# Gate and up tiles of the feed-forward block by pairs, in seven block products instead of eight

## The chip, the cores and the metric

One core of a Trainium2 chip. TensorE (PE) multiplies and writes to PSUM, VectorE (DVE) and ScalarE (ACT) read PSUM and SBUF, GpSimd (POOL) works from SBUF to SBUF, SyncE (SP) issues most of the DMAs. Each engine runs its own list of instructions in order and waits at semaphores. The metric is the device time of one execution in microseconds (us), as the median of several runs.

## The reference

Two layers of a diffusion backbone over 640 tokens (128 context, 512 latent) with 1024 channels and 2816 hidden channels. What the change touches is the second half of a layer; everything is float32.

```python
def trunk_layer(x, cond, layer_idx, p, rope, ctx):
    mod = jnp.einsum('bd,de->be', jax.nn.silu(cond), p['w_mod']) + p['b_mod']
    sh1, sc1, g1, sh2, sc2, g2 = jnp.split(mod[:, None, :], 6, axis=-1)
    h = rms_norm(x, p['norm1']) * (1 + sc1) + sh1
    ...
    x = x + g1 * (merged @ p['w_out'])
    h2 = rms_norm(x, p['norm2']) * (1 + sc2) + sh2
    ff = (jax.nn.silu(h2 @ p['w_ff_gate']) * (h2 @ p['w_ff_up'])) @ p['w_ff_down']
    x = x + g2 * ff
```

## The kernel before, in words

Activations lie channels by tokens: a tile is 128 channels by 640 tokens. A float32 product is made of three products in the type fp32r: a high part (a rounding cast) and a low part (the rest) of weight and activation, as wh·xh + wh·xl + wl·xh (`acc3`, L391 to L393). The tokens go in two parts, `SPLIT`: columns 0 to 383 and 384 to 639.

Weights come as units of 128x1024 (eight blocks of 128x128 along the 1024 inputs of one output tile). SP loads a unit into `raw`; `split_weight` has ACT cast it to `wh` (L362) and POOL subtract to `wl` (L366), in halves of 512 columns. There are four `wh` and four `wl` tiles of 1024. A unit's tiles come free when PE has made its last product (`used`), and only then is the next unit split.

A layer is the mixer (three branches), the product with `w_out` and the norm of its result, and the FFN (`ffn`). The FFN runs in three parts of 8, 7 and 7 hidden tiles (`FF_PARTS`). In a part each hidden tile takes a gate unit and an up unit, each 2 token parts by 8 blocks by 3 matmuls; ACT takes tanh (L1312), DVE multiplies (L1313, L1315, which read PSUM) and splits the result into `ah` and `al` (L383 on ACT, L384 on DVE). Then the part's product with `w_ff_down` is added to `x2` in SBUF by DVE (L1181). The first four units of a stage are made for the first token part by blocks, in four PSUM banks (`units` with `ahead`, L412), while the second token part is being normalized.

PE's list is in program order. Those of DVE, ACT and POOL are ordered by a scheduler when the program is built. Side work is fed in by `slot`, which counts the columns that PE has done. Such work is `mod_next`: it computes the modulation vector on DVE, two passes (L577) over each 128x512 tile of `w_mod`. Layer 0's runs in layer 0's mixer, the whole of layer 1's in layer 0's FFN. At the start of the program a part of it is made on PE instead (`mod_first`, L533).

## Time and profile before

| | us |
|---|---|
| median of 3 runs (2382.84 to 2386.67) | 2385.02 |
| the profiled execution | 2385.45 |
| its span, first to last instruction | 2383.7 |

The page gives each engine's busy time as a share of the span: PE 95%, DVE 59%, POOL 40%, ACT 37%. PE's records overlap, as matmuls are pipelined, so the time of one is the distance from start to start. PEclk is the granted TensorE clock: 1.00 is the upper of its two levels (2.4 GHz), 0.50 the lower (1.2 GHz). A blank between two engines' work is put down to the instruction that ended it.

### The profile page before, as it was taken

To read this page: it belongs to the slowest core of one execution; us is meant where nothing else is said; L and a number is where in the kernel's file an instruction comes from. 1 tells how busy PE (TensorE), PEld (TensorE's weight loads), DVE (VectorE), ACT (ScalarE), POOL (GpSimd) and SP (SyncE) were. 2 spreads that over 40 slices of the span, in tenths; PEclk is the share of its full clock that TensorE was granted. 3 is DMA by queue.
4 is the path that set the end of the run, shared out by engine and by line. 5 is a ranking of instruction groups with operands and counts; after the bars stand their busy time and mean duration, and the time that the engine had idled before them with its cause. 6 is when DMAs were issued, how large, how long until landed. Compare 5 with 4: busy or idle time off the path is not lost.

```text
span 2383.7 us, 42638 instructions
## 1 busy us (share of the span) xinstructions
PE 2273.8 (95%) x17060; PEld 2233.6 (94%) x17060; DVE 1417.8 (59%) x3062; ACT 879.6 (37%) x2008; POOL 956.2 (40%) x795
## 2 busy tenths in 40 slices
PE   6989899999998999999989999999999999999999
PEld 4888899999897999999979999999999989999999
DVE  5897887676956695887464657857724442222222
ACT  3444446464233322212234554464634332122221
POOL 1343644443334433444333545534333343333332
PEclk9999999999998999999999999999999999999999
DMA  7443221212511353444322222212123122222222
GB/s 286 145 130 101 79 68 53 67 54 95 198 63 54 137 177 106 151 150 149 99 101 71 79 72 72 67 48 64 48 80 112 58 71 72 80 71 73 79 80 71
DMA packets 90309, 228.25 MB, mean 96 GB/s; under 512 B 12416, under 2 KB 20480, under 8 KB 90112
## 3 DMA queue, kind: packets, MB, share of 16 engines
q1 hardware_dynamic: 85504, 218.69, 27.4%
q10 hardware_dynamic: 4608, 6.85, 0.9%
q8 instruction: 134, 2.20, 0.4%
q14 instruction: 63, 0.52, 0.1%
HBM read 213.96 MB, written 6.82 MB: 93 GB/s over the span
## 4 chain that ended last, share of the span: by engine, by line
PE 48%; DVE 7%; ACT 1%; POOL 1%; issue 1%; DMA 0%; ACTq 0%; SPq 0%; DVEq 0%; POOLq 0%
PE main L391 14%; PE main L392 14%; PE main L393 14%; PE big L412 1%; PE big L1068 1%; PE misc L1119 1%; DVE junk L577 1%; PE big L776 1%; DVE w L1000 1%; DVE ht L650 1%; DVE rs_t L472 0%; PE misc L1099 0%; DVE tg L1158 0%; DVE rs_t L473 0%; POOL ek L855 0%
## 5 line engine op out<-in xcount | busy, mean ns | idle before, releaser
L366 POOL TENSOR_TENSOR wl<-raw,wh 128x512 fp32r<-128x512 f32 x552 | 763.9, 1405 | 1142.0 <-ACT wh L362 1105.1
L362 ACT CAST wh<-raw 128x512 fp32r<-128x512 f32 x556 | 329.7, 618 | 505.2 <-PE main L392 265.4
L391 PE MATMUL main<-h2h,wh 128*128 128x256 f32 (+1 forms) x1344 | 413.2, 307 | 0.3 <-DVE tt L1313 0.3
L393 PE MATMUL main<-h2h,wl 128*128 128x256 f32 (+1 forms) x1344 | 412.8, 307 | 0.0
L392 PE MATMUL main<-h2l,wh 128*128 128x256 f32 (+1 forms) x1344 | 412.8, 307 | 0.0
L577 DVE SCALAR_TENSOR_TENSOR junk<-rawm,cond 128x512 bf16<-128x512 f32 x320 | 288.5, 902 | 37.8 <-DMA rawm<-in_w_modt_dram 33.1
L391 PE MATMUL main<-hh,wh 128*128 128x384 f32 (+1 forms) x960 | 302.4, 315 | 6.2 <-DVE rx L1200 3.5
L392 PE MATMUL main<-hl,wh 128*128 128x384 f32 (+1 forms) x960 | 297.1, 309 | 0.0
L393 PE MATMUL main<-hh,wl 128*128 128x384 f32 (+1 forms) x960 | 297.0, 309 | 0.0
L391 PEld LDWEIGHTS main<-h2h,wh 128*128 128x128 f32 x1344 | 254.6, 189 | 0.9 <-DVE tt L1313 0.5
L392 PEld LDWEIGHTS main<-h2l,wh 128*128 128x128 f32 x1344 | 254.7, 190 | 0.0
L393 PEld LDWEIGHTS main<-h2h,wl 128*128 128x128 f32 x1344 | 254.6, 189 | 0.0
L391 PE MATMUL main<-wh,hh 128*128 128x256 f32 x800 | 234.3, 293 | 5.7 <-ACT tm L461 4.0
L392 PE MATMUL main<-wl,hh 128*128 128x256 f32 x800 | 228.4, 286 | 0.0
L393 PE MATMUL main<-wh,hl 128*128 128x256 f32 x800 | 228.3, 285 | 0.0
L391 PE MATMUL main<-ah,wh 128*128 128x384 f32 (+1 forms) x704 | 219.9, 312 | 8.1 <-DVE x L1181 7.5
L392 PE MATMUL main<-al,wh 128*128 128x384 f32 (+1 forms) x704 | 218.4, 310 | 0.0
L393 PE MATMUL main<-ah,wl 128*128 128x384 f32 (+1 forms) x704 | 218.3, 310 | 0.0
L1181 DVE SCALAR_TENSOR_TENSOR x<-main,g,x 128x256 f32<-128x256 f32 (+1 forms) x192 | 78.0, 435 | 208.1 <-PE main L393 208.0
L391 PEld LDWEIGHTS main<-hh,wh 128*128 128x128 f32 x960 | 184.2, 192 | 6.9 <-DVE rx L1200 3.7
L392 PEld LDWEIGHTS main<-hl,wh 128*128 128x128 f32 x960 | 184.6, 192 | 0.1
L393 PEld LDWEIGHTS main<-hh,wl 128*128 128x128 f32 x960 | 184.2, 192 | 0.0
(276 smaller groups left out, 4698.2 us busy)
## 6 DMA issues: line engine op xcount, KB each, us to landing
raw<-in_w_dram SPq DMA_DIRECT2D x276, 512.0 KB, 3.3
rawm<-in_w_modt_dram SPq DMA_DIRECT2D x160, 256.0 KB, 4.4
rawm<-in_w_mod_dram SPq DMA_DIRECT2D x32, 256.0 KB, 5.5
x<-in_x_t_dram SPq DMA_DIRECT2D x12, 320.0 KB, 6.3
cond<-in_cond_b_dram SPq DMA_DIRECT2D x12, 256.0 KB, 4.8
qds<-qd SPq DMA_DIRECT2D x16, 160.0 KB, 2.6
x<-xd SPq DMA_DIRECT2D x8, 320.0 KB, 5.0
states<-state SPq DMA_DIRECT2D x16, 128.0 KB, 3.8
```

The source lines that it names most:

```text
L362: nc.scalar.copy(h[:, c], raw)
L366: (nc.vector if late else nc.gpsimd).tensor_sub(lo[:, c], raw, h[:, c].bitcast(F32))
L391: nc.tensor.matmul(ps, wh, xh, start=(i == 0), stop=False)
L392: nc.tensor.matmul(ps, wh, xl, start=False, stop=False)
L393: nc.tensor.matmul(ps, wl, xh, start=False, stop=(i == n - 1))
L412: self.nc.tensor.matmul(self.banks[i], a, b, start=(k == 0 and n == 0), stop=(k == KT - 1 and n == 2))
L577: nc.vector.scalar_tensor_tensor(self.sm([P, 512], "junk", 1, mybir.dt.bfloat16), raw, 1.0, cond[i, k], op0=ALU.mult, op1=ALU.mult, accum_ ...
L650: nc.vector.tensor_scalar_add(t[:, c], t[:, c], shift)
L776: nc.tensor.matmul(ps[64 * x : 64 * x + 64, o : o + 64], kk[r, ks], qq[r, qs], start=True, stop=True)
L1000: nc.vector.tensor_mul(hv(wm)[:, :, a, b], hv(x[:, 1:])[:, :, a, 1 - b], hv(sn)[:, :, a, b])
L1068: nc.tensor.matmul(S[:, x], q[:, c : c + P], k, start=(y == 0), stop=(y == 1))
L1181: nc.vector.scalar_tensor_tensor(x[:, r], ps[:, r.start - s.start : r.stop - s.start], g[:, m, i : i + 1], x[:, r], op0=ALU.mult, op1=ALU.add)
```

## The change

A gate unit and its up unit are taken together as a block matrix with two rows (gate, up: blocks A11, A12 and A21, A22, each 128 outputs by 512 inputs), and the activations as one with two columns (two token halves: B11, B21 and B12, B22). The product of the two takes eight block products; the change makes seven, in the form with sums S1 = A21+A22, S2 = S1-A11, S3 = A11-A21, S4 = A12-S2 of the weights and T1 = B12-B11, T2 = B22-T1, T3 = B22-B12, T4 = B21-T2 of the activations. For that

- the tokens are cut in equal halves of 320 everywhere, and the FFN runs in four parts of 6, 6, 5 and 5 hidden tiles; the first two hidden tiles of a layer stay as before, the other 20 are pairs (`seven`);
- weights are loaded and split in halves of 512 columns, with eight `wh` and eight `wl` tiles of that size. DVE makes S1 to S4 from the raw halves (`source`, L385, L387, L391, L398), S3 in place of A21 and S4 in place of S2; each of the seven blocks is cast by ACT (L412) and subtracted by POOL (L413);
- products of a pair are added up in PSUM where they can be, and otherwise through copies by ACT (L502, L505) and sums by DVE (L508, L514, L515, L519, L523) in tiles `e`;
- the norm keeps its result in float32 in place of x (`norm_keep`), and `combine` makes T1 to T4 and their high and low parts (L762 to L767 and L437). x itself goes to DRAM (`xd`) after `w_out`, and every part of the FFN loads it, adds and stores it;
- layer 1's modulation is cut in two. Its first part runs on PE in layer 0's FFN (`mod_later`, with `mod_first`), the rest by `mod_next` in layer 1's mixer, as layer 0's does in its own.

```diff
-FF_PARTS = ((0, 8), (8, 7), (15, 7))
-SPLIT = (slice(0, 384), slice(384, T))
-STILES = ((0, 1, 2), (3, 4))
+FF_PARTS = ((0, 6), (6, 6), (12, 5), (17, 5))
+HT = T // 2
+SPLIT = (slice(0, HT), slice(HT, T))
...
+PRODUCTS = ("A11", "S1", "S2", "A12", "S3", "S4", "A22")
...
-        self.wr = pool("wr", 2)
-        self.wh = pool("wh", 4)
-        self.wl = pool("wl", 4)
+        self.wr = pool("wr", 4)
+        self.wh = pool("wh", 8)
+        self.wl = pool("wl", 8)
...
+    def source(self, g, p):
+        nc = self.nc
+        if p in (0, 1):
+            return self.raws.pop((g, p)), 1
+        r = lambda u, i: self.raws[g + u, i]
+        if p == "A11":
+            s1 = self.sums["S1"] = self.unit("s")[:, :512]
+            nc.vector.tensor_add(s1, r(1, 0), r(1, 1))
+            nc.vector.tensor_sub(r(1, 0), r(0, 0), r(1, 0))
+            return r(0, 0), 0
+        if p == "S1":
+            s2 = self.sums["S2"] = self.unit("s")[:, :512]
+            nc.vector.tensor_sub(s2, self.sums["S1"], self.raws.pop((g, 0)))
+            return self.sums.pop("S1"), 1
+        if p in ("S2", "S4"):
+            return self.sums[p] if p == "S2" else self.sums.pop(p), 0
+        if p == "A12":
+            s4 = self.sums["S4"] = self.sums.pop("S2")
+            nc.vector.tensor_sub(s4, r(0, 1), s4)
+            return self.raws.pop((g, 1)), 1
+        return self.raws.pop((g + 1, 0 if p == "S3" else 1)), 1
...
+        key = self.jobs.popleft()
+        raw, free = self.source(*key)
+        h = self.wh.tile([P, 512], F32R, tag="wh", name=self.name("wh"))
+        lo = self.wl.tile([P, 512], F32R, tag="wl", name=self.name("wl"))
+        self.ws[key] = h, lo
+        nc.scalar.copy(h, raw)
+        low = lambda: (nc.vector if late else nc.gpsimd).tensor_sub(lo, raw, h.bitcast(F32))
         if late:
             return low
         low()
-        self.load_weight()
+        self.load_weight(free)
...
+    def seven(self, l, u, act, tmp):
+        nc = self.nc
+        g = l * N_UNITS + u
+        (e1, e16), (e5, u3) = ([t[:, s] for s in SPLIT] for t in tmp)
+        def product(ps, w, x, more):
+            h, lo = self.ws[g, w]
+            c = lambda k: slice(k * P, (k + 1) * P)
+            self.acc3(ps, [(h[:, c(k)], lo[:, c(k)], *act[x][k]) for k in range(4)], more)
+            self.used(l, u, w)
+        a, b, c = self.main()[:, :HT], self.main()[:, :HT], self.big()[:, :HT]
+        product(a, "A11", "B11", False)
+        nc.scalar.copy(e1, a)
+        self.slot(HT // 2)
+        product(b, "S1", "T1", False)
+        nc.scalar.copy(e5, b)
+        self.slot(HT // 2)
+        product(c, "S2", "T2", False)
+        nc.vector.tensor_add(e16, c, e1)
+        self.slot(HT // 2)
+        product(a, "A12", "B21", True)
+        yield 0, 0, a
+        self.slot(HT // 2)
+        product(c, "S3", "T3", True)
+        nc.vector.tensor_add(u3, c, e1)
+        nc.vector.tensor_add(e5, e5, u3)
+        yield 1, 1, e5
+        self.slot(HT // 2)
+        product(b, "S4", "B22", True)
+        nc.vector.tensor_add(e16, e16, b)
+        yield 0, 1, e16
+        self.slot(HT // 2)
+        product(c, "A22", "T4", True)
+        nc.vector.tensor_add(e1, e1, c)
+        yield 1, 0, e1
...
+    def mod_later(self, l, small, mod, scale1):
+        for c in range(4):
+            raws = []
+            first = self.mod_first(raws, c, small, mod, scale1)
+            for ks in (range(4), range(4, KT)):
+                raws += self.mod_load(c, l, ks)
+                yield
+                for _ in ks:
+                    next(first, None)
+                yield
+            for _ in first:
+                pass
...
+    def norm_keep(self, xs, rb, scale, mod, shift0, p, out):
+        nc = self.nc
+        s = SPLIT[p]
+        conds = ((0, slice(0, TC)), (1, slice(TC, HT))) if p == 0 else ((1, slice(0, HT)),)
+        for x in range(KT + 1):
+            if x < KT:
+                t = xs[x][:, s]
+                for i, c in conds:
+                    nc.vector.scalar_tensor_tensor(t[:, c], t[:, c], scale[:, x, i : i + 1], rb[:, c], op0=ALU.mult, op1=ALU.mult)
+                for i, c in conds:
+                    nc.scalar.activation(t[:, c], t[:, c], AF.Identity, bias=mod[:, shift0 + x, i : i + 1])
+                nc.scalar.copy(out[x][0][:, s], t)
+            if x >= 1:
+                (nc.vector if x % 2 else nc.gpsimd).tensor_sub(out[x - 1][1][:, s], xs[x - 1][:, s], out[x - 1][0][:, s].bitcast(F32))
...
+        t12, t4 = self.pairs("t", 4), self.pairs("t", 2)
+        act = {x: [] for x in ("B11", "T1", "T2", "B21", "T3", "B22", "T4")}
+        with self.tc.manual_schedule(engines={mybir.EngineType.DVE, mybir.EngineType.Activation}):
+            for k in range(4):
+                x, y, t = xs[k], xs[k + 4], self.unit("tf")
+                nc.vector.tensor_sub(t[:, s0], x[:, s1], x[:, s0])
+                nc.vector.tensor_sub(t[:, s1], y[:, s1], t[:, s0])
+                nc.scalar.copy(t12[k][0], t)
+                nc.gpsimd.tensor_sub(t12[k][1], t, t12[k][0].bitcast(F32))
+                nc.vector.tensor_sub(x[:, s1], y[:, s1], x[:, s1])
+                nc.vector.tensor_sub(y[:, s0], y[:, s0], t[:, s1])
+            for k in range(4):
+                x, y = xs[k], xs[k + 4]
+                d = [z[:, SPLIT[k % 2]] for z in t4[k // 2]]
+                self.split(x[:, s1], h2[k][0][:, s1], h2[k][1][:, s1])
+                self.split(y[:, s0], *d)
+                act["T4"].append(d)
...
+                    self.back, self.rate = back, 1600
+            for f in range(f, n):
+                act[f], tt = self.pairs("a", 1)[0], self.unit("tt")
+                late = {}
+                for row, p, ps in self.seven(l, u + 2 * f, act2(), [self.unit("e") for _ in range(2)]):
+                    if row == 0:
+                        gated(tt, SPLIT[p], ps)
+                    else:
+                        late[p] = ps
+                    for q in [q for q in late if (row, p) in ((0, q), (1, q)) and (q == 0 or row == 0)]:
+                        times(tt, SPLIT[q], late.pop(q), f)
...
+            def load(m):
+                if m < KT:
+                    xs[m] = self.unit("x2")
+                    nc.sync.dma_start(xs[m], self.xd[m * P : (m + 1) * P])
+            for m in range(KT if last else 2):
+                load(m)
...
+                elif p:
+                    nc.scalar.dma_start(self.xd[m * P : (m + 1) * P], xs.pop(m))
+                    load(m + 2)
...
-            mg, x2 = self.mixer(l, h, small, [self.mod_next(0, a, b, small, mod) for a, b in ((16, 36), (36, 48))] if l == 0 else None)
+            if l:
+                small, mod = later[l - 1]
+            mg, x2 = self.mixer(l, h, small, [self.mod_next(l, a, b, small, mod) for a, b in ((16, 36), (36, 48))])
...
+                nc.scalar.dma_start(self.xd[m * P : (m + 1) * P, s], x2[m][:, s])
...
-            self.ffn(l, h2, x2, g2, done, self.mod_next(l + 1, 0, 48, small, mod))
-            h = keep[1]
+                    self.queue(self.modulate(x2, acc, scale1, n_mod, 0, int(s.start > 0), keep[0]))
+            self.ffn(l, h2, act2, g2, done, self.mod_later(l + 1, n_small, n_mod, scale1))```

How it moves instructions is shown at three places. The first is VectorE's list in the middle of a part of layer 1's FFN, before: two hidden tiles. `tt` is the gated tile, `main` a PSUM bank.

```order
L1313 SCALAR_TENSOR_TENSOR tt_3799_23931<-tg_3800_23932,main_3798_23906 128x384
L1313 SCALAR_TENSOR_TENSOR tt_3799_23931<-tg_3802_23960,main_3801_23935 128x256
L1315 TENSOR_TENSOR tt_3799_23931<-tt_3799_23931,main_3806_23971 128x384
L384 TENSOR_TENSOR al_3741_23385<-tt_3799_23931,ah_3740_23384 128x384
L1315 TENSOR_TENSOR tt_3799_23931<-tt_3799_23931,main_3807_23999 128x256
L384 TENSOR_TENSOR al_3741_23385<-tt_3799_23931,ah_3740_23384 128x256
```

VectorE's list at the like place now (a pair of layer 0's first part; the pairs of both layers read alike). `e_1815` belongs to the pair before, `e_1843` to this one, `s` and `raw` are weights of the next one, and `big` is the PSUM bank of the third, fifth and seventh product.

```order
L523 TENSOR_TENSOR e_1815_9505<-e_1815_9505,big_1819_9509 128x320 [waits PE_49]
L1470 TENSOR_TENSOR tt_1798_9445<-tt_1798_9445,e_1815_9505 128x320 [waits DVE_49]
L437 TENSOR_TENSOR al_1797_9444<-tt_1798_9445,ah_1796_9443 128x320 [waits Activation_49]
L385 TENSOR_TENSOR s_1837_9642<-raw_1828_9565,raw_1831_9584 128x512 [waits DMAHW1_49,DMAHW0_49]
L437 TENSOR_TENSOR al_1797_9444<-tt_1798_9445,ah_1796_9443 128x320 [waits Activation_49]
L387 TENSOR_TENSOR raw_1828_9565<-raw_1823_9528,raw_1828_9565 128x512 [waits DMAHW7_49,DVE_49,Pool_49]
L391 TENSOR_TENSOR s_1848_9673<-s_1837_9642,raw_1823_9528 128x512
L398 TENSOR_TENSOR s_1848_9673<-raw_1836_9622,s_1848_9673 128x512 [waits DMAHW2_49,Pool_49]
L508 TENSOR_TENSOR e_1843_9656<-big_1847_9660,e_1843_9656 128x320 [waits PE_49]
L1467 SCALAR_TENSOR_TENSOR tt_1842_9655<-tt_1842_9655,main_1845_9658 128x320 [waits Activation_49]
```

Four weight sums and the PSUM sums now stand between the tile's own operations. L398 waits for POOL, and L508, the first that this pair needs, stands behind it.

The second place is TensorE's list in a pair: the end of the fourth product (A12 into `main_1845`) and the start of the fifth (S3 into `big_1847`).

```order
L443 MATMUL main_1845_9658<-h2h_1667_8454,wh_1826_9561 128x320
L443 MATMUL main_1845_9658<-h2l_1668_8455,wh_1826_9561 128x320
L443 MATMUL main_1845_9658<-h2h_1667_8454,wl_1827_9562 128x320
L443 MATMUL big_1847_9660<-h2h_1653_8440,wh_1829_9580 128x320 [waits DVE_49]
L443 MATMUL big_1847_9660<-h2l_1654_8441,wh_1829_9580 128x320
```

Before, each hidden tile's matmuls followed each other into fresh banks:

```order
L393 MATMUL main_3801_23935<-h2h_3490_21153,wl_3778_23706 128x256
L391 MATMUL main_3806_23971<-h2h_3476_21139,wh_3782_23769 128x384
L392 MATMUL main_3806_23971<-h2l_3477_21140,wh_3782_23769 128x384
L393 MATMUL main_3806_23971<-h2h_3476_21139,wl_3783_23770 128x384
L391 MATMUL main_3806_23971<-h2h_3478_21141,wh_3782_23769 128x384
```

The fifth product adds to a bank that DVE must first have read (L508), and so waits for it. ScalarE's list in the same pair, where `s_1848` is S2 of the next pair:

```order
L412 CAST wh_1849_9675<-s_1837_9642 128x512 [waits DVE_49,PE_49,Pool_49]
L502 COPY e_1843_9656<-main_1845_9658 128x320 [waits PE_49]
L505 COPY e_1844_9657<-main_1846_9659 128x320 [waits PE_49]
L412 CAST wh_1852_9694<-s_1848_9673 128x512 [waits DVE_49,Pool_49]
L412 CAST wh_1854_9712<-raw_1836_9622 128x512 [waits DMAHW2_49,PE_49,Pool_49]
```

The cast of S2 waits for its sum on DVE (L391 above). The third place is VectorE's list at the first pair of a layer: L762 to L767 are `combine`, and L1470 here waits for the last product ahead of the pairs.

```order
L763 TENSOR_TENSOR tf_1811_9460<-x2_1589_8068,tf_1811_9460 128x320 [waits DVE_49]
L1470 TENSOR_TENSOR tt_1766_9276<-tt_1766_9276,main_1789_9402 128x320 [waits PE_49]
L766 TENSOR_TENSOR x2_1585_8064<-x2_1589_8068,x2_1585_8064 128x320
L767 TENSOR_TENSOR x2_1589_8068<-x2_1589_8068,tf_1811_9460 128x320 [waits DVE_49]
L437 TENSOR_TENSOR al_1768_9278<-tt_1766_9276,ah_1767_9277 128x320 [waits Activation_49]
L762 TENSOR_TENSOR tf_1812_9467<-x2_1586_8065 128x320
```

Fourteen of `combine`'s sixteen sums, eight more `al` operations, one `al` of the tile before and one weight sum stand behind that L1470 and ahead of the first pair's L508.

## Rows read from the trace of the kernel before

**Rows 1.** Page: busy time of each engine (share of the span, x instructions).

```profile
PE 2273.8 (95%) x17060; PEld 2233.6 (94%) x17060; DVE 1417.8 (59%) x3062; ACT 879.6 (37%) x2008; POOL 956.2 (40%) x795
```

**Rows 2.** Windows: FFN of layer 0, of layer 1, gate and up there.

```profile
core 0: us, PE busy (x) PEld busy (x) DVE busy (x) ACT busy (x) POOL busy (x), PEclk, DMA share, GB/s
735.66:1229.60 493.94, 476.10 (x3184) 472.39 (x3183) 335.49 (x734) 128.50 (x263) 201.91 (x150) 0.99 0.38 129
1906.05:2380.40 474.35, 468.84 (x3176) 468.12 (x3174) 120.92 (x250) 113.69 (x231) 175.22 (x143) 0.99 0.22 75
2085.00:2183.50 98.50, 98.50 (x675) 98.50 (x674) 22.34 (x41) 26.77 (x55) 36.65 (x28) 1.00 0.23 75
```

**Rows 3.** Groups of instructions: busy us, mean ns | idle before, released by.

```profile
L366 POOL TENSOR_TENSOR wl<-raw,wh 128x512 fp32r<-128x512 f32 x552 | 763.9, 1405 | 1142.0 <-ACT wh L362 1105.1 <-issue 27.5 <-PE big L1010 7.8
L362 ACT CAST wh<-raw 128x512 fp32r<-128x512 f32 x556 | 329.7, 618 | 505.2 <-PE main L392 265.4 <-issue 188.7 <-PE main L393 22.7
...
L1315 DVE TENSOR_TENSOR tt<-tt,main 128x384 f32<-128x384 f32 x40 | 22.0, 551 | 66.3 <-PE main L393 66.3
L1315 DVE TENSOR_TENSOR tt<-tt,main 128x256 f32<-128x256 f32 x44 | 18.4, 419 | 28.3 <-PE main L393 28.1
```

**Rows 4.** Single lines: duration in ns, min/median/max, and forms.

```profile
L384 DVE TENSOR_TENSOR al<-tt,ah x88: 411/786/1496, 763.9 to 2332.8; 128x384 fp32r<-128x384 f32 x44, 128x256 fp32r<-128x256 f32 x44
L384 DVE TENSOR_TENSOR fl<-f,fh x8: 822/825/826, 90.8 to 1304.3; 128x640 fp32r<-128x640 f32 x8
L366 POOL TENSOR_TENSOR wl<-raw,wh x552: 1259/1296/1992, 21.5 to 2356.4; 128x512 fp32r<-128x512 f32 x184
L1181 DVE SCALAR_TENSOR_TENSOR x<-main,g,x x192: 341/473/486, 676.8 to 2380.6; 128x256 f32<-128x256 f32 x128, 128x128 f32<-128x128 f32 x64
```

**Rows 5.** Timeline of POOL and DVE from 125 us: start, duration.

```profile
125.03 0.69 DVE L577 SCALAR_TENSOR_TENSOR junk<-rawm,cond 128x512 bf16<-128x512 f32 x1
125.16 6.89 POOL L366 TENSOR_TENSOR wl<-raw,wh 128x512 fp32r<-128x512 f32 x4 [10.00 <-ACT wh L362]
...
125.76 1.66 DVE L577 SCALAR_TENSOR_TENSOR junk<-rawm,cond 128x512 bf16<-128x512 f32 x1
...
127.46 1.66 DVE L577 SCALAR_TENSOR_TENSOR junk<-rawm,cond 128x512 bf16<-128x512 f32 x1
```

**Rows 6.** Windows around three waits of PE (columns as in rows 2).

```profile
1892.70:1897.18 4.48, 0.28 (x4) 0.08 (x2) 4.24 (x11) 1.14 (x2) 2.70 (x3) 0.82 0.38 118
1897.18:1902.43 5.25, 5.25 (x20) 4.64 (x21) 3.90 (x13) 2.31 (x6) 0.91 (x2) 0.50 0.28 99
1911.30:1916.20 4.90, 0.30 (x3) 0.04 (x1) 4.55 (x10) 0.83 (x2) 3.75 (x7) 0.99 0.32 107
1916.20:1922.90 6.70, 6.70 (x22) 6.70 (x23) 2.20 (x12) 0.00 (x0) 0.00 (x0) 0.50 0.01 4
252.70:257.21 4.51, 0.06 (x2) 0.00 (x1) 4.51 (x5) 1.06 (x3) 2.85 (x2) 0.62 0.36 87
257.21:260.62 3.41, 3.41 (x16) 3.41 (x17) 3.41 (x6) 2.98 (x6) 1.47 (x1) 0.50 0.02 5
```

**Rows 7.** Windows: both mixers from their fifth unit, then both layers' first down products.

```profile
59.40:671.50 612.10, 577.08 (x4725) 566.78 (x4725) 483.44 (x1056) 284.06 (x686) 262.04 (x217) 0.98 0.30 98
1257.65:1841.60 583.95, 570.51 (x4725) 561.08 (x4725) 355.83 (x747) 280.47 (x677) 251.06 (x218) 0.99 0.22 72
859.20:922.10 62.90, 57.85 (x387) 56.52 (x387) 43.90 (x109) 9.43 (x17) 22.87 (x16) 1.00 0.41 140
2028.70:2085.00 56.30, 56.30 (x386) 56.30 (x386) 10.52 (x25) 9.45 (x17) 20.43 (x16) 1.00 0.23 76
```

**Rows 8.** Timeline of PE at the start, where L533 runs between other products.

```profile
38.64 0.33 PE L412 MATMUL big<-hh,wl 128*128 128x384 f32 x1
38.90 0.42 PE L533 MATMUL misc<-rawm,cond 128*32 128x128 f32 x8
39.26 0.45 PE L412 MATMUL big<-hh,wh 128*128 128x384 f32 x1
```

More of the change, by code (lines that the diff above doesn't have):

```diff
@@ L361, in split_weight @@
-        for raw, c in parts:
-            nc.scalar.copy(h[:, c], raw)
-        def low():
-            for raw, c in parts:
-                (nc.vector if late else nc.gpsimd).tensor_sub(lo[:, c], raw, h[:, c].bitcast(F32))
+        key = self.jobs.popleft()
[4 more added lines that the diff above has]
+        nc.scalar.copy(h, raw)
@@ new lines, in combine @@
+    def combine(self, xs, h2):
+        nc = self.nc
+        s0, s1 = SPLIT
+        t12, t4 = self.pairs("t", 4), self.pairs("t", 2)
[15 more added lines that the diff above has]
+                act["T4"].append(d)
+        for k in range(4):
+            for name, pair, s in (
+                ("B11", h2[k], s0), ("T3", h2[k], s1), ("B21", h2[k + 4], s0), ("B22", h2[k + 4], s1), ("T1", t12[k], s0), ("T2", t12[k], s1)
+            ):
+                act[name].append([z[:, s] for z in pair])
+        return act
@@ L1296, in mixer, with ffn @@
         return mg, x2
[L1298 removed]
+    def ffn(self, l, h2, act2, g2, done, back=None):
         nc = self.nc
@@ L1302, in ffn @@
         for fp, (_, n) in enumerate(FF_PARTS):
[L1303 to L1316 removed]
+            last = fp == len(FF_PARTS) - 1
@@ new lines, in ffn, with gated, times @@
+            act = {}
+            def gated(tg, s, ps):
+                nc.scalar.activation(tg[:, s], ps, AF.Tanh, scale=0.5)
+                nc.vector.scalar_tensor_tensor(tg[:, s], tg[:, s], 1.0, ps, op0=ALU.add, op1=ALU.mult)
+            def times(tg, s, ps, f):
+                nc.vector.tensor_mul(tg[:, s], tg[:, s], ps)
+                self.split(tg[:, s], act[f][0][:, s], act[f][1][:, s])
+            f = 0
+            if fp == 0:
+                tt = {}
+                for i, ps, s in self.units(l, range(u, u + AHEAD), h2, AHEAD):
+                    f = i // 2
+                    if i % 2 == 0:
+                        if s.start == 0:
+                            tt[f], act[f] = self.unit("tt"), self.pairs("a", 1)[0]
+                        gated(tt[f], s, ps)
+                    else:
+                        times(tt[f], s, ps, f)
+                f = AHEAD // 2
+                if back is not None:
+                    self.back, self.rate = back, 1600
```

193 lines of the change are left out of this document (103 added, 90 removed).

## The prediction

> **What bounds the kernel now.** I read the page first: PE is busy for 95% of the span, every other engine for at most 59% [rows 1]. Then the windows by stage. In layer 1's gate and up products PE has no idle time at all, and POOL and DVE do 37 and 22 us of work in 98.5 us [rows 2]. The window holds seven hidden tiles, 7 x 96 = 672 matmuls of 320 columns in the mean, so one takes 0.1466 us. There, only fewer matmuls or PE kept waiting can change the time. Next I looked for what the new work will run on. The groups and single lines give the durations [rows 3, 4], and the timeline shows how DVE and POOL meet [rows 5]: a DVE operation with both inputs in SBUF takes 0.69 us alone, and 1.66 while POOL subtracts; POOL's four subtractions then take 1.72 each instead of 1.29. They take turns. An `al` operation of 256 columns runs from 411 ns to 1496, while L1181, which reads PSUM, never takes over 486 ns [rows 4]. So a DVE operation of two SBUF inputs that finds POOL at work waits about 1.0 us (1.66 - 0.69; 1.50 - 0.42), and one that reads PSUM does not wait.
>
> **The change part by part.**
>
> *Matmuls removed.* Twenty pairs a layer, each with 12 matmuls fewer (84 for 96): 480 x 0.1466 = **-70.3 us**. A pair takes 14.07 us before and 12.31 after, if PE never waits; its seven products take 1.76 each. (The Trainium skill, "TensorE: Matmul & The Clock Gate", section "Back-to-back issue gap", gives the distance as columns / 2.4 GHz + 2.5 ns. That is 135.8 ns for 320 columns, and by it the term would be -65.2 us; the row is 11 ns longer, so the row decides.)
>
> *Work added to a pair.* POOL now subtracts seven halves instead of four, 7 x 1.29 = 9.0 us [rows 4]. DVE gets four weight sums of 512 columns (0.69 each) and five sums of 320. From 0.42 for 256 and 0.55 for 384 I take 0.49 for 320, whatever is read [rows 3], if nothing is in the way. No engine's own sum exceeds 12.3 us. What matters is the order.
>
> *The chain in a pair.* PE's fifth product adds to a bank that DVE must have read (L508). On DVE, L508 stands behind all of this since the seventh product of the pair before: L523, L1470, two `al`, L385, L387, L391, L398. And L398 overwrites S2, so it waits for POOL's subtraction of S2, which waits for ACT's cast, which waits for L391. From the end of the last product: L523, L1470 and two `al` 4 x 0.49, the sums L385, L387 and L391 3 x 0.69, together 4.0; cast 0.62; POOL 1.29; L398 0.69; L508 0.49; some eight hand-overs between engines at an estimated 0.1: 7.9 us. PE has four products to do meanwhile, 7.0 us. Without any turn lost to POOL the wait is 0.9 us a pair, and that is the lower bound. With turns lost: of the seven DVE operations ahead of the cast, six have two SBUF inputs, while POOL has the next pair's A11 and S1 to subtract; two lost turns, 2.0 us. The third is at L398: when S2 is done, the cast of A12 behind it is done too, and POOL goes on with it while L398 is being released; 1.0 more. Sum 10.9 us, less 7.0: **3.8 us** that PE waits. The upper bound, with a fourth lost turn or a weight that lands late, is 5. The order of instructions has this chain 12 times a layer (2, 4, 3 and 3 in the four parts, where two more pairs follow whose weights must be made); 24 x 3.8 = **+91 us**. (The Trainium skill, "SBUF — State Buffer", section "SBUF: two separate sides", calls the shared pair of ports an exclusive lock, held for a whole instruction by whichever starts first. The trace agrees on the lock. A wait that starts anywhere in a subtraction of 1.29 us would last 0.65 in the mean, and by that 3.8 would be 2.8 and the term +67; the rows show 1.0, as POOL tends to be just starting.)
>
> *The clock after each wait.* PE waited 4.5, 4.9 and 4.5 us in three places, and the granted clock was 0.50 for 5.25, 6.7 and 3.4 us behind that [rows 6]. Half of these is lost: 1.7 to 3.3 us. A wait of 3.8 is near those, so I take 2.0 (bounds 0 and 3.3): 24 x 2.0 = **+48**.
>
> *First and last pairs of a part.* Six more pairs (the first of a part) have only the end of the chain, from the second product on: copy 0.45, cast 0.62, POOL 1.29, L398 0.69, L508 0.49 and hand-overs against PE's 3.5; 0.4 or, with a lost turn, 1.4. I take 0.9: **+5**. At a part's end, L523, L1470, cast and `al` with one lost turn and hand-overs are 3.2 us, of which the next product's earlier blocks cover 1.8 to 2.2: 1.2 x 8 = **+10** (bounds 4 and 16). Before, these products ran without idle time in layer 1 [rows 7].
>
> *The first pair of a layer.* Behind the L1470 that ends the units ahead, DVE has 23 operations of 0.49, one of 0.69, and L508: 12.9 us with L1470 itself. With seven lost turns (the weights of four units and four of `combine`'s own subtractions come due on POOL) 19.9, less 7.0: 12.9 and a clock loss of 2.0, **+30** for both layers. Bounds: 11 without lost turns, 46 if POOL's longer subtractions each cost a turn.
>
> *Modulation moved.* In layer 0's mixer, where L577 runs, the same stretch took 612.1 us; in layer 1's, without it, 584.0 [rows 7]. Now it runs in both: I take **+25** of the 28 (bounds 15 and 30). Layer 0's FFN loses it: its first down products took 62.9 us against 56.3. I count this difference for two of the three parts, **-12** (the third part's end also has the next norm). In its place 32 groups of L533 go to PE. At the start such a group lies between two matmuls that begin 0.62 us apart instead of 0.17 [rows 8], and the next is late too; 0.55 each, **+18**, less where they fall into a wait.
>
> *Norms.* Equal halves give the first half's norm more cover (96 matmuls of 320 columns, 14.1 us, for 11.5) and the second half's less (14.1 for 16.6), and `norm_keep` has fewer DVE operations. PE waits 4.5 and 4.9 us there [rows 6]: **-6** for both layers (bounds 0 and -8). x through DRAM I cost at nothing: DMA is at 0.22 of its share in layer 1's FFN [rows 2], and tiles are asked for two ahead of use; if that cover is gone, PE waits for a landing in each down part.
>
> *Sum:* -70.3 + 91 + 48 + 5 + 10 + 30 + 25 - 12 + 18 - 6 = +139. The profiled execution took 2385.45 us (span 2383.7, 1.75 outside it), 0.4 over the median: 2385.45 + 139 = **2524 us**.
>
> **The rivals.** *Turns are not lost where I put them (faster).* If DVE's chain falls between POOL's subtractions, the wait is 0.9, the clock stays up, and the ends and the first pairs cost their lower bounds: -70 + 22 + 0 + 4 + 11 + 20 - 12 + 18 - 8 = -15, 2370 us. It speaks for it that the subtraction waits for the cast in 1105 of its 1142 idle us [rows 3], so POOL is not always there; against it, that POOL must now work 9 of 12.3 us. It decides where the wait falls below about 1.5 us a pair.
> *The chain is shorter, and the clock stays up.* Two us a pair: -70 + 48 + 3 + 8 + 24 + 25 + 6 - 6 = +38, 2423 us. For it: L385 stands ahead of L523 in three pairs, and the scheduler may have left L391 early; against it, the wait at L398.
> *All bounds are high.* 5.0 and 3.3 a pair: -70 + 199 + 8 + 14 + 46 + 28 + 8 = +233, 2618 us. For it: a raw half can only be loaded when its buffer is free, and the last sums would then wait for a landing.
> *The waits come, but the clock stays up.* Shorter waits of PE in other places may leave it at 1.00; then the sum is 139 - 48 = +91, 2476 us. Against it stand all three rows [rows 6]. It lies in my own case's range.
>
> **How the numbers follow.** My forecast (waits of 3 to 4.5 us, with or without a part of the clock loss, 2460 to 2580 us) has 0.52; the shorter chain 0.2; all high 0.12; the faster case 0.12; 0.04 lies between it and the shorter chain, of which 0.03 within 0.2% of 2385, which is about what a measurement of this kernel can tell from no change. So faster 0.12, same 0.03, slower 0.85. The range goes from the shorter chain's low side, 2405, to the high case, 2615, and leaves out some 0.2.
>
> **What would show it.** In the changed profile, right: the distance of pairs in the middle of a part is 16 to 19 us, at a part's end 12.3 to 13; PE's fifth product waits for DVE L508, and L508's predecessor L398 for POOL; DVE operations of 512 columns show 0.69 and 1.7; the clock is 0.50 in slices of the FFN; layer 1's FFN takes about 530 us and its mixer 610. Wrong: pairs at 12.3 to 13.5 us throughout, L398 without a wait, a clock of 1.00 in the FFN, or layer 1's mixer at 584.

## The result and the profile after

The changed kernel takes 2534.67 us (median of 4 runs, 2533.32 to 2536.93), the kernel before, beside it, 2383.93: ratio 1.0631, 95% interval 1.0613 to 1.065. That is slower, 11 us above the forecast of 2524.

The page, busy time of each engine and the granted clock by slices (compare [rows 1]):

```profile
PE 2289.4 (90%) x16858; PEld 2225.4 (88%) x16858; DVE 1668.8 (66%) x3362; ACT 1028.6 (41%) x2272; POOL 1132.7 (45%) x903
...
PEclk9999999999998999999989999999999989899999
```

The windows of both FFNs, then of layer 1's and layer 0's mixer from the fifth unit (compare [rows 2, 7]), columns as there:

```profile
735.59:1286.60 551.01, 482.14 (x3210) 467.06 (x3209) 305.65 (x513) 194.75 (x389) 278.71 (x206) 0.93 0.36 117
1991.54:2529.90 538.36, 468.15 (x2940) 457.24 (x2938) 291.22 (x465) 180.53 (x356) 268.99 (x197) 0.93 0.30 100
1311.86:1929.40 617.54, 584.63 (x4726) 571.69 (x4725) 474.64 (x1045) 289.52 (x688) 266.70 (x225) 0.97 0.29 92
56.50:675.00 618.50, 580.99 (x4726) 569.58 (x4725) 479.76 (x1059) 289.70 (x689) 261.80 (x219) 0.98 0.31 99
```

The FFNs are longer by 57 and 64 us, layer 1's mixer by 34, layer 0's by 6. Some 12 us come back outside these windows, mostly in the two `w_out` products and at the mixers' starts. PE is idle in 70 us of each FFN, and the clock there fell from 0.99 to 0.93.

A pair in layer 1's second part: of DVE's timeline an L1470 and the stretch from L387 to L508, POOL's and ACT's beside it, then PE.

```profile
2165.15 1.07 DVE L1470 TENSOR_TENSOR tt<-tt,e 128x320 f32<-128x320 f32 x1
...
2167.55 0.68 DVE L387 TENSOR_TENSOR raw<-raw,raw 128x512 f32<-128x512 f32 x1
2168.15 1.78 DVE L391 TENSOR_TENSOR s<-s,raw 128x512 f32<-128x512 f32 x1
2172.02 1.73 DVE L398 TENSOR_TENSOR s<-raw,s 128x512 f32<-128x512 f32 x1 [2.09 <-POOL wl L413]
2173.68 0.48 DVE L508 TENSOR_TENSOR e<-big,e 128x320 f32<-128x320 f32 x1
...
2168.03 1.35 POOL L413 TENSOR_TENSOR wl<-s,wh 128x512 fp32r<-128x512 f32 x1 [2.16 <-ACT wh L412]
2170.72 1.27 POOL L413 TENSOR_TENSOR wl<-s,wh 128x512 fp32r<-128x512 f32 x1 [1.33 <-PE main L443]
2171.94 2.94 POOL L413 TENSOR_TENSOR wl<-raw,wh 128x512 fp32r<-128x512 f32 x2
...
2170.02 0.62 ACT L412 CAST wh<-s 128x512 fp32r<-128x512 f32 x1 [1.41 <-DVE s L391]
...
2174.21 0.64 PE L443 MATMUL big<-h2h,wh 128*128 128x320 f32 x1 [3.50 <-DVE e L508]
```

L391 loses a turn to POOL (1.78 for 0.68), ACT casts the sum at 2170.02, POOL subtracts S2 until 2171.99, and only then does L398 begin, which loses the next turn to POOL's A12 (1.73). L508 ends at 2174.16, and PE, idle for 3.50 us, starts its fifth product at 2174.21. (The profile puts POOL's 1.33 us ahead of S2 down to a PE product, whose modelled end falls just there; the cast ended at 2170.64, and for the same wait in an earlier pair, at 2062.96, the profile names the cast.) The waits of the whole execution (us in total, times, longest) have one such line for PE and one for L398:

```profile
PE big L443 <- DVE e L508: 82.5, 24, 3.8
...
DVE s L398 <- POOL wl L413: 90.8, 40, 6.1
...
DVE s L385 <- DMA raw<-in_w_dram: 28.8, 13, 3.1
DVE x L1337 <- DMA x<-xd: 17.9, 7, 3.0
```

Three windows: that wait, what follows it, and the rest of the pair.

```profile
2170.71:2174.21 3.50, 0.01 (x2) 0.00 (x1) 2.19 (x3) 1.30 (x3) 3.49 (x3) 0.97 0.23 75
2174.21:2177.61 3.40, 3.40 (x13) 3.40 (x14) 0.34 (x1) 0.06 (x1) 0.68 (x1) 0.53 0.48 154
2177.61:2182.80 5.19, 5.19 (x37) 5.19 (x36) 3.69 (x7) 2.74 (x5) 3.91 (x3) 1.00 0.07 21
```

In the 3.40 us at the lower clock PE starts 13 matmuls where 23 would fit, a loss of 1.5 us; in other pairs it was 6.8 us, a loss of 2.4 to 2.9. This pair has a distance of 17.53 us to the next; a pair without the wait takes 12.32.

### The profile page after: what moved, and what is told of

The parts are those of the page before. It is cut to its first block, busy times and chain, and to the rows that moved or that the text cites. A ratio compares the mean times of both kernels' runs of the same rounds, so it can differ in the third digit from the quotient of the medians.

```text
span 2533.3 us, 44691 instructions
## 1 busy us (share of the span) xinstructions
PE 2289.4 (90%) x16858; PEld 2225.4 (88%) x16858; DVE 1668.8 (66%) x3362; ACT 1028.6 (41%) x2272; POOL 1132.7 (45%) x903
## 4 chain that ended last, share of the span: by engine, by line
PE 57%; DVE 21%; issue 7%; POOL 5%; DMA 4%; ACT 3%; SPq 0%; ACTq 0%; POOLq 0%; DVEq 0%
PE main L443 40%; PE big L443 9%; DVE junk L682 6%; POOL wl L413 3%; DMA raw<-in_w_dram 2%; PE big L1224 2%; DVE s L398 2%; PE misc L1275 1%; DMA x<-xd 1%; POOL ek L1011 1%; DVE w L1156 1%; ACT wh L412 1%; PE big L932 1%; PE misc L1255 1%; DVE mod L686 1%
## 5 line engine op out<-in xcount | busy, mean ns | idle before, releaser
L413 POOL TENSOR_TENSOR wl<-raw,wh 128x512 fp32r<-128x512 f32 x552 | 770.7, 1406 | 901.3 <-ACT wh L412 783.4
L412 ACT CAST wh<-raw 128x512 fp32r<-128x512 f32 x556 | 340.0, 620 | 448.9 <-PE main L443 378.1
L443 PE MATMUL main<-hh,wh 128*128 128x320 f32 x960 | 304.0, 317 | 2.9 <-DVE aT L1394 2.9
L443 PE MATMUL main<-hl,wh 128*128 128x320 f32 x960 | 299.8, 312 | 4.5 <-POOL hl L804 4.1
L443 PE MATMUL main<-hh,wl 128*128 128x320 f32 x960 | 298.7, 311 | 0.0
L413 POOL TENSOR_TENSOR wl<-s,wh 128x512 fp32r<-128x512 f32 x120 | 163.7, 1364 | 217.3 <-ACT wh L412 185.4
L443 PE MATMUL main<-wh,hh 128*128 128x256 f32 x800 | 235.5, 294 | 12.1 <-DVE rx L1356 7.8
L443 PE MATMUL main<-ah,wh 128*128 128x320 f32 x704 | 220.7, 314 | 23.9 <-DVE x L1337 15.0
L443 PE MATMUL main<-wh,hl 128*128 128x256 f32 x800 | 229.7, 287 | 0.0
L443 PE MATMUL main<-wl,hh 128*128 128x256 f32 x800 | 229.7, 287 | 0.0
L1337 DVE SCALAR_TENSOR_TENSOR x<-main,g,x 128x128 f32<-128x128 f32 (+2 forms) x240 | 96.3, 435 | 198.4 <-PE main L443 180.1
L443 PE MATMUL main<-al,wh 128*128 128x320 f32 x704 | 218.3, 310 | 0.9
L443 PE MATMUL main<-ah,wl 128*128 128x320 f32 x704 | 217.5, 309 | 0.0
L443 PEld LDWEIGHTS main<-hl,wh 128*128 128x128 f32 x960 | 182.4, 190 | 6.8 <-POOL hl L804 6.1
L443 PEld LDWEIGHTS main<-hh,wh 128*128 128x128 f32 x960 | 182.5, 190 | 3.6 <-DVE aT L1394 3.3
L443 PEld LDWEIGHTS main<-hh,wl 128*128 128x128 f32 x960 | 182.3, 190 | 0.0
L412 ACT CAST wh<-s 128x512 fp32r<-128x512 f32 x120 | 74.4, 620 | 252.5 <-PE big L443 131.6
L443 PE MATMUL main<-h2h,wh 128*128 128x320 f32 x544 | 175.6, 323 | 0.0
L443 PE MATMUL main<-h2l,wh 128*128 128x320 f32 x544 | 174.3, 320 | 0.0
L443 PE MATMUL main<-h2h,wl 128*128 128x320 f32 x544 | 173.3, 319 | 0.0
L443 PEld LDWEIGHTS main<-wh,hh 128*128 128x128 f32 x800 | 157.0, 196 | 15.1 <-DVE rx L1356 8.2
```

The source lines that it names most:

```text
L412: nc.scalar.copy(h, raw)
L413: low = lambda: (nc.vector if late else nc.gpsimd).tensor_sub(lo, raw, h.bitcast(F32))
L443: mm = lambda w, x, first=False, last=False: nc.tensor.matmul(ps, w, x, start=first and not more, stop=last, skip_group_check=more)
L1337: nc.vector.scalar_tensor_tensor(x[:, r], ps[:, r.start - s.start : r.stop - s.start], g[:, m, i : i + 1], x[:, r], op0=ALU.mult, op1=ALU.add)
```

## Experiments

Labels of the lines are those of the changed kernel; in some variants they are shifted. The kernel before, measured beside each group of them, was at 2386 to 2387 us each time.

### The wait for POOL, and the place behind it

`s4_own` keeps the order and takes the overwriting away; `e16_first` keeps the overwriting and changes the order of two instructions.

```diff
-            s4 = self.sums["S4"] = self.sums.pop("S2")
-            nc.vector.tensor_sub(s4, r(0, 1), s4)
+            s4 = self.sums["S4"] = self.unit("s")[:, :512]
+            nc.vector.tensor_sub(s4, r(0, 1), self.sums.pop("S2"))
```

> S4 goes into a tile of its own, so L398 no longer waits for POOL's subtraction of S2; its place on DVE, ahead of L508, stays. Theory (DVE stands still at L398 for POOL, and PE's fifth product stands behind that): of the chain that I had put at 10.9 us per pair the cast (0.62), POOL's subtraction (1.29), the turn lost at L398 (1.0) and some three hand-overs (0.1 each) leave the path. 7.7 us stay, against 7.0 that PE has to do. PE waits 0 to 1.5 us instead of 3.8 before the fifth product, 0.7 in the middle. 24 x 3.1 = 74 us less, and up to 24 x 2.2 = 53 more if the half clock behind the waits goes with them: 2407 to 2460, 2420 in the middle. Rival 1 (the overwrite doesn't matter: it is DVE's seven operations ahead, with their lost turns): the wait stays at 2.5 us or more, time 2505 or more. Rival 2 (the waits go, but the clock falls behind short ones just the same): half clock stays at some 4 us a pair, time about 2460.

```diff
-            self.used(l, u, w)
+            if w != "S2":
+                self.used(l, u, w)
...
-        nc.vector.tensor_add(e16, c, e1)
+        with self.tc.manual_schedule(engines={mybir.EngineType.DVE}):
+            nc.vector.tensor_add(e16, c, e1)
+            self.used(l, u, "S2")
```

> Only the order on DVE: L508 (in this kernel's numbering L510) stands ahead of the sum S4 instead of behind it; S4 still overwrites S2 and still waits for POOL. Theory (it is the place behind the wait that costs): L508 is done 4.0 us of sums, two lost turns and 0.5 after the last product of the pair before, 6.8 us against PE's 7.0, so PE's wait before the fifth product falls from 3.8 to 0 to 0.5. But the wait for POOL is still there and now holds up the sums that free the bank for the seventh product (L514): the sum S4 ends some 10.4 us after the last product, L1467 and L514 bring it to 11.6, and PE is there at 10.6. So a new wait of about 1.0 us (0 to 2) ahead of the seventh product. 24 x (2.8 + 2.0 of clock) = 115 us less: 2420, 2385 to 2450. Rival 1 (DVE's work altogether, wherever the wait stands): the wait only moves, 3 us or more ahead of the seventh product, time above 2500. Rival 2 (POOL's seven subtractions bound the pair): pairs stay at 17 us or more, with PE waiting for wl.

Measured: `s4_own` 2422.69 us (ratio to before 1.0158, 1.014 to 1.0176), `e16_first` 2426.42 (1.0171, 1.0154 to 1.0188). Both take some 110 us off. PE's waits for the fifth product in `s4_own`, the windows of two pairs in the middle and of both FFNs, then L398's waits and a pair's window in `e16_first`:

```profile
PE big L443 <- DVE e L508: 12.0, 21, 0.8
...
2115.33:2128.56 13.23, 12.58 (x87) 12.32 (x85) 10.85 (x16) 6.52 (x14) 9.74 (x8) 1.00 0.23 81
2128.56:2141.81 13.25, 12.58 (x86) 12.32 (x85) 10.88 (x16) 6.52 (x14) 9.75 (x8) 1.00 0.23 80
737.58:1233.10 495.52, 461.75 (x3212) 447.18 (x3211) 299.00 (x516) 194.59 (x390) 277.82 (x206) 0.97 0.38 131
1935.88:2418.67 482.79, 448.55 (x2940) 436.94 (x2938) 282.52 (x467) 180.83 (x357) 268.26 (x198) 0.98 0.32 112
```

```profile
DVE s L398 <- POOL wl L413: 50.7, 34, 1.8
...
2129.58:2143.17 13.59, 13.06 (x87) 12.32 (x85) 11.23 (x17) 6.43 (x13) 10.10 (x8) 1.00 0.23 78
```

DVE and POOL do the same work as before, and the pair goes from 17.5 to 13.3 us. So it was neither the sums as such nor POOL's seven subtractions, but one wait with something urgent queued behind it; either edit alone is enough. In `e16_first` L398 still waits 50.7 us in all, and PE hardly notices. Waits of up to 0.8 us leave the clock at 1.00. Of the 112 us that `s4_own` saves, 70 are PE's waits (82.5 to 12.0). The other 41 are, as far as the traces tell, the clock: in the changed kernel the matmuls at 0.50 behind these waits lose some 45 us, in `s4_own` no matmul behind them ran at 0.50. Its FFNs have a clock of 0.97 and 0.98 where the changed kernel's have 0.93.

### What the rest of the change costs

`no_pairs` computes every gate and up tile as before the change and leaves `combine` out.

```diff
-            pairs.update(range(u + (0 if fp else AHEAD), u + 2 * n, 2))
+            pass
...
-                for row, p, ps in self.seven(l, u + 2 * f, act2(), [self.unit("e") for _ in range(2)]):
+                for i, ps, s in self.units(l, [u + 2 * f, u + 2 * f + 1], h2):
...
```

> All hidden tiles as before the change, with eight block products, and without the sums of the activations; equal halves, four parts, x through DRAM, the norm that keeps its result and the moved modulation stay. Theory: what the change brings besides the pairs is the sum of my terms for it, +25 - 12 + 18 - 6 = +25, and what I had at nothing, x through DRAM (15 to 20 us of PE's waits for L1337 in the down parts of the changed kernel's trace) and the equal halves in the mixers (6 us each in layer 0, where no modulation was added): 2385 + 25 + 18 + 12 - 5 = 2435, 2420 to 2450. By the terms on record alone 2410. Rival (the pairs cost little beside their waits for L508, and the rest of the change is what makes it slower): 2470 or more.

`no_mod1` gives layer 1's mixer no modulation to work on.

```diff
+            if l:
+                nc.vector.tensor_copy(mod[:, 16:48], small[:, S_BM + 16 : S_BM + 48, None].to_broadcast([P, 32, 2]))
-            mg, x2 = self.mixer(l, h, small, [self.mod_next(l, a, b, small, mod) for a, b in ((16, 36), (36, 48))])
+            mg, x2 = self.mixer(l, h, small, None if l else [self.mod_next(l, a, b, small, mod) for a, b in ((16, 36), (36, 48))])
```

> Leaves out: layer 1's modulation in its mixer (its vector is the bias alone there); everything else is as changed. Theory (the 128 passes over w_mod on DVE cost the mixer 28 us, as they do in layer 0): layer 1's mixer takes 590 us instead of 618, and the whole 28 less, 2507 (2500 to 2515). Rival (the mixers are longer by the equal halves): it falls by 10 us or less.

Measured: `no_pairs` 2416.14 us (1.0129, 1.0114 to 1.0144), nearer to the 2410 of my terms than to the 2435 that I had corrected them to. Its FFNs, and then layer 1's mixer in `no_mod1`:

```profile
736.87:1229.46 492.59, 483.75 (x3452) 478.76 (x3451) 148.09 (x309) 142.01 (x278) 179.65 (x142) 0.99 0.39 131
1938.16:2412.15 473.99, 469.86 (x3180) 468.93 (x3178) 133.34 (x262) 127.58 (x244) 170.35 (x133) 0.99 0.34 113
```

```profile
1321.30:1911.91 590.61, 574.93 (x4727) 565.31 (x4725) 351.66 (x751) 286.12 (x680) 254.33 (x222) 0.99 0.22 72
```

Without the pairs both FFNs take what they took before [rows 2]: x through DRAM, four parts, and modulation on PE instead of DVE together cost nothing there. The 30 us are in the mixers, which are 6 and 39 us longer (618.4 and 623.2), less some 12 that come back outside. In the changed kernel the modulation is 27 us of layer 1's mixer (617.54 to 590.61). As a whole `no_mod1` was only 13 us faster than the changed kernel (2521.79), and that was my own edit: the scheduler put its one new instruction, the copy of the bias, at the program's start, where DVE stood at it until layer 1's `small` had landed.

```profile
41.71 0.20 DVE L1606 COPY mod<-small 128x64 f32<-128x64 f32 x1 [13.14 <-DMA small<-in_small_dram]
```

The first mixer began 14.5 us later for it; 27 less 14 is the 13. `no_pairs` and `s4_own` also say what the pairs were worth without the big wait: nothing yet, 2416 against 2423. The 70 us of fewer matmuls were still eaten up elsewhere: in `s4_own`, from start to start, the middle pairs are together some 19 us above 12.32 each, the first pairs of the two layers 33, and the eight down parts 27 above those of `no_pairs`.

### Where the other 70 us went

`both` has the two first edits together. Each of the next three adds one edit: the first half of `combine` is issued earlier, x is loaded earlier, and there are six raw buffers for four.

> The two edits of the first experiments together: S4 in its own tile, and L508 ahead of L398 on DVE. In the kernel with S4 in its own tile PE still waits 0.7 to 1.0 us before the fifth product of the middle pairs (pairs of 13.0 to 13.25 us), in the one with the other order 0.3 there and 0.7 more a pair further on (13.0 to 13.6). Theory (both rests are the two ends of one queue on DVE, the operation ahead of L508 and the wait behind it): pairs of 12.4 to 12.7 us, 26 x 0.6 = 16 us less than with S4 in its own tile: 2407 (2400 to 2415). Rival (POOL's turns make the rest): pairs stay at 13.0 or more, 2418 or more.

```diff
...
+                    if i == 0 and s.start:
+                        act2(True)
                 f = AHEAD // 2
...
```

> As the run of both edits, and the first half of combine (T1, T2, their high and low parts, and the float32 of T3 and T4) is issued after the first product of the second token half instead of after the last one; the second half, which overwrites h2, stays. Theory (the first pair of a layer loses 3.4 us ahead of its second product and 11.3 in it, to POOL's low part of T, and works at half clock behind that: a pair of 25.4 us and a gap of 3.4 where 12.3 would do): T1 and T2 are ready when PE comes, and what stays are eight low parts on DVE ahead of L508, some 8 to 10 us against PE's 7.0. The first pair then takes 13 to 17 us. 12 to 15 us less in each layer, 27 together (20 to 31): 2380. Rival (POOL is late there because the weights of four units and three weight sums come due, wherever T stands): under 12 us less.

```diff
             for f in range(f, n):
+                if f == n - 1:
+                    for m in range(2):
+                        load(m)
...
```

> As the run before, and the first two loads of x of every FFN part are issued ahead of the part's last pair instead of behind it. Theory (on SP's queue they stand behind loads of weights, which wait for POOL to free a raw half, and they land 2 to 3 us after DVE wants the first): DVE's first L1337 of a part has no wait for the load; PE's gap of some 0.9 us at the third product goes; 7 x 0.9 = 6 us less (3 to 9). What stays of 5 us a part is DVE standing at weight sums for a raw half. Rival (x is all of it, as the load is named in the waits): 15 us or more less.

```diff
-UNITS = 58
+UNITS = 57
...
-        self.wr = pool("wr", 4)
+        self.wr = pool("wr", 6)
```

> As the run before, and six raw buffers instead of four for weight halves (paid by one tile of 128x640 less in the other pool, 57 for 58). Theory (in a down part DVE stands twice at the first weight sum of the next pairs, L385, until a raw half lands that could only be loaded when a buffer came free; L1337, behind it, frees PE's bank late: gaps of 1.2 and 1.0 us): the halves land in time, 7 x 2.2 = 15 us less (8 to 18), the down parts of layer 1 at 43 to 44 and 36 us instead of 47 and 40. Rival (the scheduler puts the sums so early that they only wait longer): no change, or slower by the lost tile in the mixers.

Measured: 2425.93, 2419.24, 2417.58 and 2402.92 us (ratios 1.0164, 1.0142, 1.0129, 1.0063, each within 0.0025). Three of the four forecasts were too hopeful.

- `both`: no gain. Its middle pairs run at 13.2 us like those of `s4_own`, with the wait ahead of the fourth product now, for ACT's copy; the rival's bound holds, its cause, POOL's turns, is not shown by this.
- `both_early`: 7 us for 27; the rival's bound was 12 in each layer. PE's waits around the first pair of layer 1, first of the changed kernel, then here:

```profile
PE main L443 <- ACT th L764: 5.8, 4, 3.2
PE main L443 <- POOL tl L765: 4.8, 4, 1.4
```

```profile
PE main L443 <- ACT e L503: 4.8, 1, 4.8
PE main L443 <- DVE tt L1476: 3.3, 1, 3.3
```

T is ready now, but the pair still takes 23.7 us, as its products now wait for DVE's and ACT's other queued work (L503 and L1476 are L502 and L1470 of the changed kernel).
- `both_early_x`: 2 us for 6, within the runs' scatter. DVE's waits for x fall from 17.4 us in all to 1.6, so the load was late as thought, and it cost little.
- `wr6u57`: 15 us, the number forecast, but not from where I had it: the eight down parts give back only 6.5, and DVE's waits at L385 for a raw half only fall from 30.3 to 25.4 us. Layer 1's mixer is 6.2 shorter (618.42 to 612.19), but that need not be the buffers: with six of them it took 616.7 in `late_t3` and 615.1 in `act_order`, with four 615.4 in `both_early`, and layer 0's stayed at 620.

Three more edits tried to use the rest. `late_t3` spreads `combine` over four products and puts T3 and T4 behind L508; `act_order` puts ACT's copies ahead of its casts; `mod_down` moves 40 modulation tiles into layer 0's down parts.

```diff
...
+                    if s.start:
+                        act2(i)
...
+        if "last" in act:
+            act.pop("last")()
...
```

> As the run with six raw buffers, and the sums of the activations are spread out: the operations of T1 and T2 are issued by fours, one share behind each of the four products of the second token half, with DVE in the order of the program there; the parts of T3 and T4 (eight casts, eight low parts) come behind the first pair's L508 instead of ahead of it. Theory (the first pair's rest, 23.2 us and a gap of 3.5 where 12.3 would do, is a queue on DVE: L1476, which frees a bank, behind weight sums, and L508 behind eight low parts): the gap ahead of S1 falls from 3.5 to 1 to 2 us, the wait before the fifth product from 5.8 to 0 to 1.5, and the half clock behind them goes: 7 to 12 us less in each layer, 2403 - 20 = 2383 (2378 to 2390). Rival (POOL is the bound there: four low parts of 1.6 us and eight of 1.3 in some 14 us): the waits move to the first pair's S1 or S2, under 5 us less in each layer, 2393 or more.

```diff
-        nc.scalar.copy(e1, a)
+        with self.tc.manual_schedule(engines={mybir.EngineType.Activation}):
+            nc.scalar.copy(e1, a)
+            self.used(l, u, "A11")
...
```

> As the run before, and only ScalarE's order is changed: a pair's copies out of PSUM (e1, e5) stand ahead of the casts of the next pair's S1 and the like, not behind them. Theory (the pairs of 13.2 us in the middle lose 0.4 to 0.7 us ahead of the fourth product, which adds to the bank that ACT copies; the copy stands behind the cast of S1, and that waits for DVE's L385): pairs at 12.4 to 12.8, 24 x 0.5 = 12 us less, 2371 (2368 to 2378). Rival (POOL's and DVE's turns close the circle of a pair at 13.2 us anyway): the wait turns up at the fifth product again, under 4 us less.

```diff
+                if not last:
+                    next(side, None)
                 self.slot(s.stop - s.start)
...
```

> As the run before, and 40 of the 64 tiles of w_mod that layer 1's mixer works through go to layer 0's FFN, one to each product of its first three down parts, where DVE has little else; 58 tiles again in the pool (one small buffer less pays for it). Theory (the mixer is longer by 28 us for 64 tiles, and in a down part two passes of 0.7 us fit beside an L1337 of 0.5 in each 2.6 us of PE): layer 1's mixer 17 us shorter, the three down parts 0 to 8 us longer; 2371 - 17 + 4 = 2358 (2353 to 2366), 1% below the kernel before. Rival (L1337 comes late behind the passes and PE runs out of its two banks): the down parts 15 us longer or more, no gain.

Measured: 2407.63, 2412.2 and 2401.75 us (1.0084, 1.0103, 1.0057). `late_t3` gains nothing: the first pair is shorter from its second product on (19.6 us), but the waits went ahead of that product (4.9 us for DVE's L1470) and ahead of the first (3.1 for L1467). `act_order` moves PE's wait from the fourth product (0.4 us) to the fifth (0.7); pairs stay at 13.2. In `mod_down` layer 1's mixer gives 21.7 us back (615.07 in `act_order`, 593.39 here; 17 forecast), but the three down parts are 15 us longer, its rival's bound; the whole is 10 us faster, where the rival had no gain. The first of these parts, in `act_order` and in `mod_down`:

```profile
842.10:889.22 47.12, 44.74 (x327) 43.17 (x329) 18.82 (x38) 8.69 (x16) 16.19 (x13) 1.00 0.58 193
```

```profile
837.02:890.54 53.52, 47.51 (x327) 44.72 (x329) 46.44 (x104) 10.89 (x20) 18.09 (x13) 0.97 0.74 255
```

DVE has 66 operations more there and is busy for 27.6 us more, 46 of 53.5; PE's banks come free late.

### The last kernel

`last` collects what helped and adds two edits: S1 and S3 of the next pair are made in DVE's idle time, and a part's first down product is made in both token halves by turns.

```diff
+        with self.tc.manual_schedule(engines={mybir.EngineType.DVE}):
+            nc.vector.tensor_add(u3, c, e1)
+            nc.vector.tensor_add(e5, e5, u3)
+            self.ahead(0)
...
+            for p in range(2):
+                outs[0, p] = self.main()[:, :HT]
+                down(0, p, range(n - 1))
+            for p in (1, 0):
+                down(0, p, (n - 1,))
...
```

> All that helped so far (S4 in its own tile, L508 ahead of L398, ScalarE's copies first, the first half of combine early in one piece, x loaded ahead of the last pair, six raw buffers, 40 modulation tiles in the down parts), and two new edits. First, DVE makes the next pair's sums S1 and S3 (L385, L387) in its idle time between the fifth and the seventh product, instead of in the queue behind the seventh. Theory (the pairs of 13.25 us are a circle on DVE: from tanh of the sixth product to L508 it has no idle time, 7.9 us with four turns lost to POOL, and PE needs 7.0): some 0.8 to 1.4 us leave the circle, pairs of 12.3 to 12.6, 24 x 0.8 = 19 us less. Second, the two token halves of a part's first down product take turns: all blocks but the last tile's of both halves first, then the last tile's. Theory (PE waits 1.2 + 0.4 or 1.6 + 0.4 us at each part's end for the last tile's high and low part): 4.4 us of cover instead of 2.2, 8 x 1.6 = 13 us less. From 2402 with the first pairs as they were 2 us a layer shorter: 2366 (2358 to 2378), below the kernel before. Rival (POOL takes the turns there instead, and the circle closes at 13.2 us as in the runs before): only the second edit counts, 2385.

Measured: 2387.59 us in 11 runs, ratio 1.0004 (0.9995 to 1.0013): all that the change had lost, and nothing won. It is the rival's number (2385): the middle pairs are no shorter than before, and the eight down parts are 15 us shorter than in `mod_down`, which speaks for the second edit alone; the two were not run apart. Two pairs in the middle:

```profile
2104.20:2117.65 13.45, 12.60 (x87) 12.33 (x86) 12.35 (x16) 6.40 (x13) 10.77 (x8) 1.00 0.26 80
2117.65:2131.10 13.45, 12.60 (x87) 12.33 (x86) 11.42 (x15) 6.51 (x13) 10.76 (x8) 1.00 0.25 79
```

The fifth product no longer waits in any pair of the middle, and PE stands 0.9 us ahead of the fourth instead, for an ACT copy that is queued behind a cast of DVE's result. DVE is now busy for 11.9 of 13.45 us in the mean, against 10.9 in `s4_own`, for the same operations: made at another time, they lose more turns to POOL. The five orders of DVE and ACT that were tried all end at 13.2 to 13.6 us.

## Why the prediction came out right

**Matmuls removed** (-70.3): right; pairs without a wait have the 12.32 us forecast.

**The chain in a pair** (+91): right in its mechanism, its place and its size. 24 waits, nearly all of 3.8 us between the last start of one product and the first of the next, 82.5 us by the profile's count and 86 from start to start. In layer 1 the pairs with a wait are 17.5 to 18.9 us apart (16 to 19 forecast). In the pair shown the lost turns are 0.6 us at L1470 and 1.1 each at L391 and L398, for three of 1.0; the hand-overs, for whose 0.1 each no row was given, are 0.03 to 0.09. `s4_own` and `e16_first` show that L508's place behind a wait for POOL is the cause; the rival that DVE's chain fits between POOL's subtractions is out.

**The clock after each wait** (+48): right; the 45 us above, or 41 as what `s4_own` leaves. The rival of waits without a clock loss (2476) is out.

**First pairs of a part** (+5): 0; all six have no wait there. **Part ends** (+10) **and x through DRAM** (0): mis-sized. A down part of six tiles takes 47.24 us in layer 1, against 42.40 for the same product in `no_pairs` (the two lines below); over the eight parts it is 27 us.

```profile
2104.11:2151.35 47.24, 43.71 (x292) 42.46 (x291) 17.41 (x36) 8.44 (x15) 15.99 (x13) 1.00 0.47 160
2031.83:2074.23 42.40, 42.40 (x292) 42.40 (x291) 10.98 (x25) 7.98 (x14) 15.81 (x13) 1.00 0.53 176
```

The last tile's high and low part are some 1.5 of 5 us in a part, about what I had for part ends; the rest is L1337, which frees PE's two banks, standing behind the landing of x (3.0 us) and behind weight sums that wait for a raw half (L385, 28.8 us in all). I had named the cover of x and not the queue: SP issues its loads behind those of weights that wait for POOL. In layer 1 of `no_pairs` the same loads were in time; in layer 0 two were late. That the weight sums hold the rest is read from the trace only: the two edits aimed at these waits brought 2 us (`both_early_x`) and, in the down parts, 6.5 (`wr6u57`).

**The first pair of a layer** (+30): right in size, 25.4 and 24.70 us and a gap of 3.4 each for 12.3, together 32; wrong in place, so the size is luck. PE waited in and ahead of the second product for ACT's and POOL's parts of T, not at L508. Making T earlier (`both_early`) took these waits away, and others, behind the same full queues, came in their place.

**Modulation moved** (+25), **-12 + 18** and **norms** (-6), +25 together: `no_pairs` has +30 for them. (The term of -12 is twice 6.6, so 13.) The modulation is 27 in layer 1's mixer, the FFNs cancel out. Not foreseen: both mixers are some 6 us longer without any added work (618.50 for 612.10 in layer 0, 590.61 in `no_mod1` for 583.95 in layer 1), and some 12 us come back outside. Whether the equal halves do that was not tried; and 6 us is not far above the scatter, as the same mixer of layer 1 takes 612 to 623 us from kernel to kernel.

From `no_pairs` the sum closes: +30 - 70 + 86 + 45 + 27 + 32 = +150, by which the profiled execution is longer. So 2524 was the right sum from mostly right terms. The part ends with x were 17 too low and the moved work 5; the waits, the clock and the first pairs of a part were 13 too high, and that these partly cancel is luck.

## What to carry to other kernels

Fewer matmuls are worth their price only if the engines that feed them have room in the same microseconds: here 12 matmuls less per pair brought four weight sums, five sums of products and three subtractions to two engines that take turns at SBUF. Before judging such a change by busy shares, look for an instruction that waits for another engine and has something urgent behind it in its queue; a second buffer or a swap of two rows was worth 110 us of 150. What then remains is a ring of short waits, and taking one away only shows the next.
